# Twenty-two product units made on the spot and thirty-six from sums kept in DRAM, in place of forty-four made on the spot

## The chip, the cores and the metric

The kernel runs on one core of one Trainium2 chip. The metric is the device time of one execution in microseconds (us). Three runs of the kernel before took 2204.83, 2204.56 and 2203.43 us; the median is 2204.56 us.

A core has five engines that run their own instruction streams side by side and wait for each other through semaphores: TensorE (PE in the profile, with its weight loads as PEld), VectorE (DVE), ScalarE (ACT), GpSimd (POOL) and SyncE (SP). SP does nothing here but issue transfers (DMA) from device memory (DRAM) into the core's on-chip memory. Each engine takes its instructions strictly in the order in which they stand in its stream. Matmuls add into a second on-chip memory, PSUM.

## The reference, cut to what matters

The reference is a two-layer encoder trunk with 256 tokens and a model width of 2048, all in float32. Layer 0 mixes by neighbourhood attention, layer 1 by a gated short convolution. Each layer ends with a gated MLP of inner width 5632.

```
for i in range(2):
    a = rms_norm(h, mix_norm[i])
    if i == 0:
        q, k, v = split(a @ w_qkv, 3);  mixed = neighbourhood_softmax(q, k, v) @ w_o
    else:
        gb, gc, x = split(a @ w_in, 3); mixed = (gb * conv3(gc * x)) @ w_out
    h = h + mixed
    g, u = split(conv3(rms_norm(h, ffn_norm[i]) @ w_up) + conv_b, 2)
    h = h + (silu(g) * u) @ w_down
out = rms_norm(h, final_norm)
```

What counts for the time is nine large products with weights: `w_qkv` (q and k part `wqk`, v part `wv`), `w_o`, twice `w_up` and `w_down`, `w_in` (`wsc`) and `w_out` (`wscout`).

## The kernel before, in words

**Three matmuls for one product.** TensorE multiplies in the rounded form fp32r. To keep float32 accuracy, `parts` splits every weight chunk of 128x1024 numbers into a rounded part `hi` (ScalarE, line 139) and the rest `lo` (VectorE, line 140), and the activations are kept as such pairs too. A product is then hi·hi + hi·lo + lo·hi.

**Two kinds of stages.** In the stages `Phase` (q and k, `w_up`, `w_in`) the weights are stationary: an item is two tiles of 128 outputs, each over sixteen k tiles from two weight chunks. Line 185 does hi weights against both parts of the activation (512 wide) and line 193 lo weights against the hi part (256 wide). With `intro=3` the first three outputs are done one chunk at a time, so that the stage can start on the first eight k tiles of its input. In the stages `Tokens` (`w_o`, `w_down`, `w_out`) the activations are stationary and the weights move, 512 wide, in two groups `g` of eight output tiles. A pair of k tiles in a group is a 2x2 problem of 128 tokens by 512 outputs.

**Eight products or seven.** A plain pair does its 2x2 problem in eight products (`product`, lines 375 to 377, three matmuls each). A unit of seven does it in seven, in the manner of Strassen (`seven`): it needs sums of activations (`make_forms`, on GpSimd) and of weights (`sums`, lines 149 to 152: four VectorE additions of 128x512, then the split). Four of its products collect in four PSUM accumulators `mu`; at the end of a group `combine` (lines 409 to 417) folds those into the residual stream `h`. The plans at the top of the file say in which order the pairs of a group come and which are units of seven: 44 in all, ten in each first half of an MLP, seven in each second half, six in `w_out`, four in `w_o`.

**What sets the order.** The program text emits the work item by item. All weight chunks of the whole program stand in one list, `chunks`; `prep_to` loads them on SP through a ring of five buffers `raw` and splits them into six buffers `hi` and six `lo`, four chunks ahead of the item that TensorE works on (`AHEAD`). Per engine the instructions are then put into an order at build time, by the due times that the framework reckons, and this order is fixed when the kernel runs.

**The hand-overs.** After `w_o`, after the first layer's MLP and after `w_out` a `Tokens` stage ends and a `Phase` stage follows that needs the normalized result. `to_norm` adds the last groups into `h` (line 273), takes their squares, transposes `h` on TensorE (line 284), scales it to the new activations `a` (ScalarE line 225, VectorE line 226), works out the reciprocal root of the mean square (`token_factor`, lines 260 to 269 and 290 to 294) and spreads it over the partitions (`spread_factor`: line 300 on TensorE, line 301 copies it to `rstd`). Meanwhile TensorE does the intro items of the next stage with the eight k tiles that are ready, and it needs a8 to a15, the last eight, to go on. The last stage ends in `finale` and the final norm (`last_evac`).

Of the kernel before, what the change touches and what calls it, by code (L numbers as in the profile page):

```python
# [22 lines left out]
P = 128  # L23
# [20 lines left out]
S_FIRST = ((ORDER, (1, 3, 5, 7, 9), 3), ((0, 2, 1, 4, 3, 6, 5, 8, 7, 10, 9), (1, 3, 5, 7, 9), 6))  # L44

S_SECOND = (((0, 2, 1, 4, 3, 6, 5, 8, 7, 9, 10), (1, 3, 5, 7), 1), (ORDER, (3, 5, 7), 1))
S_OUT = (1, 3, 5)
S_ATT = (((0, 1, 2, 6, 3, 7, 4, 5), (6, 7), 1),) * 2
# [19 lines left out]
def trunk(ctx, tc, xT, par, bias, wqk, wv, wo, wsc, wscout, wup, wdown, out):  # L68
# [8 lines left out]
    ep = ctx.enter_context(tc.tile_pool(name="ends", bufs=1))  # L77

# [35 lines left out]

    def prep_to(n):
        while len(prepped) < min(n, len(chunks)):
            src, w, kind = chunks[len(prepped)]
            raw = wp.tile([P, CH * P], F32, name="raw", tag="raw", bufs=5)
            if kind == "rows":
                nc.sync.dma_start(out=raw[:, :w], in_=src)  # L120
                prepped.append(parts(raw[:, :w]) + (raw,))
                continue

            nc.sync.dma_start(out=raw.rearrange("p (f c) -> p f c", f=4), in_=src.rearrange("f p c -> p f c"))
            r = raw.rearrange("p (f k c) -> p f k c", f=4, c=P)
# [17 lines left out]
    def sums(l, r):  # L143

        t13 = wp.tile([P, CH * P], F32, name="raw", tag="raw", bufs=5)
        t24 = tp.tile([P, CH * P], F32, name="t24", tag="qk")
        v13, v24 = (x.rearrange("p (k f c) -> p f k c", f=4, c=P) for x in (t13, t24))
# [3 lines left out]
        add(out=v24[:, :, 0, :], in0=v13[:, :, 0, :], in1=r[:, :, 1, :])  # L151
        add(out=v24[:, :, 1, :], in0=v24[:, :, 0, :], in1=l[:, :, 1, :])  # L152
        return parts(r[:, :, 1:2, :]), parts(t13), parts(t24)

    class Phase:
# [3 lines left out]
        def __init__(self, w, fts, nk, src, evac, intro=0, step=CH):  # L159
# [8 lines left out]
            for two, ks in order:  # L168
# [4 lines left out]
                ends.append(len(chunks))  # L173

# [128 lines left out]
    class Tokens:  # L303
# [4 lines left out]
        def __init__(self, w, nk, src, evac, plan, forms, halves=0):  # L308
# [4 lines left out]
            for g, (order, sset, _) in enumerate(plan):  # L313
                for i in order:
# [3 lines left out]
                    if g == KT // 8 - 1 and k >= nk - halves:  # L318
# [3 lines left out]
                        chunks.extend(((left, 8 * P, "cols"), (right, 8 * P, "cols")))  # L322
                        continue
                    chunks.append((left, 8 * P, "cols"))
                    if i in sset:
                        chunks.append((right, 8 * P, "sums"))
                        items.append((self, g, c + 1, k, k, k + 2))
                        ends.append(c + 2)
                    else:
                        chunks.append((right, 8 * P, "cols"))  # L330
# [48 lines left out]
        def seven(self, g, c, k0):  # L379
# [7 lines left out]
            left, (w22, t13, t24) = prepped[c - 1], prepped[c]  # L387
# [3 lines left out]
            for ps, x, w, j in ((a, raw(0, 0), left, 0), ("11", raw(1, 0), left, 1), ("12", s4, w22, 0),  # L391
                                (e, s1, t13, 0), (f, s3, t13, 1), (b, s2, t24, 0), ("21", raw(1, 1), t24, 1)):
# [28 lines left out]
    def make_forms(xe, xo, place=None):  # L421

        if place is None:
            n = form_at[0] = (form_at[0] + 1) % 5
            y = tp.tile([P, 8 * P], F32R, name="sf", tag=("sf", "vv", "sf", "vv", "qk")[n], bufs=2)
            place = y[:, :4 * P], y[:, 4 * P:]
# [164 lines left out]
    def sc_evac(f, ps):  # L591
# [11 lines left out]
        else:  # L603
# [3 lines left out]
            if j % 2 == 0:  # L607
                sc_of["even"] = t
            elif j // 2 in S_OUT:
                yforms[j // 2] = make_forms(sc_of["even"], t)  # L610
# [113 lines left out]
    def mlp(layer, a, evac):  # L724
        for half in range(2):
            act, forms = [None] * HALF, {}
            lo = half * HALF
            Phase(wup[layer], [f for j in range(lo, lo + HALF) for f in (2 * j, 2 * j + 1)], KT, a, up_evac(layer, act, forms, (S_SECOND if half else S_FIRST)[0][1]),
                  intro=0 if half else 3)
            Tokens(wdown[layer, half], HALF, act, evac if half else residual, S_SECOND if half else S_FIRST, forms,  # L730
                   halves=4 if half and layer else 0)

    for g in range(NH // 4):
        Phase(wqk, range(8 * g, 8 * g + 8), KT, a0, qk_evac, intro=0 if g else INTRO, step=STEP)
        Values(g, a0)
    Tokens(wo, KT, oT, to_norm(1, a1), S_ATT, oforms)
    mlp(0, a1, to_norm(2, a2))
    Phase(wsc, range(3 * KT), KT, a2, sc_evac, intro=3)
# [136 lines left out]
```

## Time and profile before

| | us |
|---|---|
| median of 3 runs | 2204.56 |
| lowest and highest run | 2203.43, 2204.83 |
| profiled execution, span from first to last instruction | 2203.5 |

Stages, by the timeline of TensorE:

| stage | kind | from, to (us) | units of seven |
|---|---|---|---|
| q, k, v and attention, four groups | Phase with values and softmax between | 0 to 309 | none |
| `w_o` | Tokens | 309 to 395 | 4 |
| MLP of layer 0 | Phase, Tokens, Phase, Tokens | 395 to 1116 | 10 and 7 |
| `w_in` | Phase | 1116 to 1378 | none |
| `w_out` | Tokens | 1378 to 1470 | 6 |
| MLP of layer 1 | Phase, Tokens, Phase, Tokens | 1470 to 2190 | 10 and 7 |

The page of the profile covers one execution. Times are in microseconds unless marked ns. A row of groups names line, engine, operation and tile, then the count, the busy time, the mean time of one, and the idle time of the engine just before them with what ended it. A row of the timeline gives start, duration, engine, line, operation and operands, and in brackets the idle time before it. Matmuls overlap, so a row of eight of them takes less than eight times a single one's duration.

### The profile page before, as it was taken

To read this page: it belongs to the slowest core of one execution; us is meant where nothing else is said; L and a number is where in the kernel's file an instruction comes from. 1 tells how busy PE (TensorE), PEld (TensorE's weight loads), DVE (VectorE), ACT (ScalarE), POOL (GpSimd) and SP (SyncE) were. 2 spreads that over 40 slices of the span, in tenths; PEclk is the share of its full clock that TensorE was granted. 3 is DMA by queue.
4 is the path that set the end of the run, shared out by engine and by line. 5 is a ranking of instruction groups with operands and counts; after the bars stand their busy time and mean duration, and the time that the engine had idled before them with its cause. 6 is when DMAs were issued, how large, how long until landed. Compare 5 with 4: busy or idle time off the path is not lost.

```text
span 2203.5 us, 31950 instructions
## 1 busy us (share of the span) xinstructions
PE 2191.7 (99%) x11776; PEld 1900.1 (86%) x11776; DVE 1752.7 (80%) x2677; ACT 1274.6 (58%) x1900; POOL 71.4 (3%) x115
## 2 busy tenths in 40 slices
PE   9999999999999999999999999999999999999998
PEld 8888888888888888888888888888888888888886
DVE  8777678877788987778876666898777898777887
ACT  7555556665655565565555445566556556665554
POOL 0000000000000000000000000000000000000000
PEclk9999999999999999999999999999999999999999
DMA  7565546555556755555665555565555566555564
GB/s 259 191 198 180 172 150 211 190 191 191 191 172 196 226 200 186 191 190 185 200 196 189 187 191 183 174 224 180 190 187 184 177 212 219 191 191 192 170 203 134
DMA packets 214605, 421.00 MB, mean 191 GB/s; under 512 B 13488, under 2 KB 142640, under 8 KB 214448
## 3 DMA queue, kind: packets, MB, share of 16 engines
q1 hardware_dynamic: 213072, 418.33, 58.4%
q8 instruction: 92, 1.51, 0.3%
q10 hardware_dynamic: 1376, 0.63, 0.1%
q14 instruction: 65, 0.53, 0.1%
HBM read 416.81 MB, written 2.10 MB: 190 GB/s over the span
## 4 chain that ended last, share of the span: by engine, by line
PE 96%; DVE 1%; DMA 1%; ACT 1%; issue 0%; SPq 0%; DVEq 0%; ACTq 0%
PE mm L185 41%; PE mm L193 22%; PE mm L375 8%; PE mm L376 8%; PE mm L377 8%; PE mu L375 2%; PE mu L377 2%; PE mu L376 2%; PE mm L570 1%; PE mm L572 1%; PE mm L571 1%; DMA raw<-in_wqk 1%; PE tr L284 1%; DVE lo L140 0%; PE tr L525 0%
## 5 line engine op out<-in xcount | busy, mean ns | idle before, releaser
L140 DVE TENSOR_TENSOR lo<-raw,hi 128x1024 fp32r<-128x1024 f32 (+1 forms) x836 | 973.1, 1186 | 188.3 <-PE mm L193 123.4
L139 ACT CAST hi<-raw 128x1024 fp32r<-128x1024 f32 (+1 forms) x836 | 845.7, 1019 | 368.9 <-PE mm L377 121.8
L185 PE MATMUL mm<-a,hi 128*128 128x512 f32 x4096 | 961.7, 391 | 0.9 <-ACT hi L139 0.4
L185 PEld LDWEIGHTS mm<-a,hi 128*128 128x128 f32 x4096 | 759.2, 188 | 153.8 <-DVE a L226 2.0
L193 PEld LDWEIGHTS mm<-a,lo 128*128 128x128 f32 x4096 | 512.9, 192 | 11.9
L193 PE MATMUL mm<-a,lo 128*128 128x256 f32 x4096 | 518.0, 283 | 0.0
L375 PE MATMUL mm<-hi,act 128*128 128x512 f32 x696 | 271.4, 390 | 0.0
L376 PE MATMUL mm<-lo,act 128*128 128x512 f32 x696 | 271.1, 389 | 0.0
L377 PE MATMUL mm<-hi,act 128*128 128x512 f32 x696 | 270.8, 389 | 0.0
L238 ACT COPY corr<-mm 128x256 f32<-128x256 f32 x256 | 94.8, 372 | 240.0 <-PE mm L193 240.0
L254 DVE SCALAR_TENSOR_TENSOR conv<-pad,pt,conv 128x256 f32<-128x256 f32 x384 | 184.8, 482 | 43.8 <-ACT conv L252 28.8
L252 ACT ACTIVATE conv<-pad,pt 128x256 f32<-128x256 f32 x176 | 105.6, 601 | 145.8 <-DVE pad L244 145.8
L377 PEld LDWEIGHTS mm<-hi,act 128*128 128x128 f32 x696 | 130.6, 188 | 27.2
L375 PEld LDWEIGHTS mm<-hi,act 128*128 128x128 f32 x696 | 130.7, 188 | 26.8
L376 PEld LDWEIGHTS mm<-lo,act 128*128 128x128 f32 x696 | 130.7, 188 | 26.6
L239 DVE TENSOR_TENSOR corr<-mm,corr 128x256 f32<-128x256 f32 x256 | 106.9, 418 | 2.0 <-ACT corr L238 1.9
L218 DVE TENSOR_TENSOR act<-conv,act 128x256 fp32r<-128x256 f32 x88 | 37.4, 425 | 85.8 <-ACT act L217 85.8
L244 DVE TENSOR_TENSOR pad<-corr,rstd 128x256 f32<-128x256 f32 x176 | 74.0, 421 | 0.1
L139 ACT CAST hi<-t 128x1024 fp32r<-128x1024 f32 x44 | 46.4, 1054 | 39.6 <-DVE t L152 26.5
L140 DVE TENSOR_TENSOR lo<-t,hi 128x1024 fp32r<-128x1024 f32 x44 | 53.8, 1222 | 4.8 <-ACT hi L139 3.7
L149 DVE TENSOR_TENSOR raw<-raw 128x512 f32<-128x512 f32 x44 | 30.4, 690 | 33.2 <-DMA raw<-in_wdown 28.9
L570 PE MATMUL mm<-hi,a 128*128 128x512 f32 x128 | 50.5, 394 | 0.0
(157 smaller groups left out, 1464.0 us busy)
## 6 DMA issues: line engine op xcount, KB each, us to landing
raw<-in_wup SPq DMA_DIRECT2D x352, 512.0 KB, 4.9
raw<-in_wdown SPq DMA_DIRECT2D x176, 512.0 KB, 4.5
raw<-in_wsc SPq DMA_DIRECT2D x96, 512.0 KB, 4.9
raw<-in_wqk SPq DMA_DIRECT2D x56, 512.0 KB, 4.7
raw<-in_wv SPq DMA_DIRECT2D x32, 512.0 KB, 4.5
raw<-in_wo SPq DMA_DIRECT2D x32, 512.0 KB, 4.5
raw<-in_wscout SPq DMA_DIRECT2D x32, 512.0 KB, 4.4
raw<-in_wqk SPq DMA_DIRECT2D x16, 256.0 KB, 5.1
```

The lines of the kernel that those rows point to most:

```text
L139: nc.scalar.copy(out=hv, in_=r)
L140: nc.vector.tensor_sub(out=lv, in0=r, in1=hv.bitcast(F32))
L185: nc.tensor.matmul(self.ps[ft], lhsT=prepped[i][0][:, o:o + P], rhs=self.src[k], start=k == 0, stop=False)
L193: nc.tensor.matmul(self.ps[ft][:, S:], lhsT=prepped[i][1][:, o:o + P], rhs=self.src[k][:, :S], start=False, stop=k == self.nk - 1)
L238: nc.scalar.copy(out=corr, in_=ps[:, S:])
L239: nc.vector.tensor_add(out=corr, in0=ps[:, :S], in1=corr)
L244: nc.vector.tensor_mul(out=dst, in0=both(ps), in1=rstd)
L252: nc.scalar.activation(c, x[:, 1:S + 1], AF.Identity, scale=w[1], bias=b)
L254: nc.vector.scalar_tensor_tensor(out=c, in0=x[:, tap:tap + S], scalar=w[tap], in1=c, op0=ALU.mult, op1=ALU.add)
L375: nc.tensor.matmul(ps, lhsT=xh, rhs=wh, start=start, stop=False)
L376: nc.tensor.matmul(ps, lhsT=xh, rhs=wl, start=False, stop=False)
L377: nc.tensor.matmul(ps, lhsT=xl, rhs=wh, start=False, stop=stop)
```

## The change

There are 58 units of seven in place of 44, in two kinds. Twenty-two ("S") make their weight sums on the spot as before; their second sum tile is now written back into the right chunk's buffer in place of a tile of its own. Thirty-six ("D") take sums that were made earlier. Each half of a D unit's sums is a **job**: one load of 512 KB on SP, four additions of 128x2x128 in place on VectorE, and two stores of 256 KB on ScalarE's queue, which are issued when three more chunks have been prepared. The jobs stand in the chunk lists of the `Phase` stages: four in each group of q and k but the first, twelve in each `w_up` stage, twenty in `w_in`, 72 in all, spread evenly over the items. Their results lie in DRAM until the `Tokens` stage loads them, two chunks of 512 KB each, which are split like weights; of the pair's own right chunk it then loads half.

```
+def plan(text, due):
+    words = text.split()
+    return (tuple(int(x[1:]) for x in words), {int(x[1:]): x[0] for x in words if x[0] != "P"}, due)
-S_FIRST = ((ORDER, (1, 3, 5, 7, 9), 3), ((0, 2, 1, 4, 3, 6, 5, 8, 7, 10, 9), (1, 3, 5, 7, 9), 6))
-S_SECOND = (((0, 2, 1, 4, 3, 6, 5, 8, 7, 9, 10), (1, 3, 5, 7), 1), (ORDER, (3, 5, 7), 1))
-S_OUT = (1, 3, 5)
-S_ATT = (((0, 1, 2, 6, 3, 7, 4, 5), (6, 7), 1),) * 2
+S_FIRST = (plan("P0 D1 P2 S3 D4 P5 D6 S7 P8 D9 P10", 3), plan("P0 P2 D1 S3 D4 P5 D6 S7 P8 P10 D9", 6))
+S_SECOND = (plan("P0 P2 D1 S3 D4 P5 D6 S7 D8 P9 P10", 1), plan("P0 P1 P2 D3 S4 P5 D6 S7 D8 P9 P10", 1))
+S_OUT = (plan("P0 D1 P2 S3 D4 D5 P6 P7", 1),) * 2
+QK_JOBS, UP_JOBS, SC_JOBS = 4, 12, 20
+S_ATT = (plan("P0 P1 P2 S6 P3 S7 P4 P5", 1),) * 2
...
     def prep_to(n):
...
+            while stores and stores[0][0] <= len(prepped):
+                stores.pop(0)[1]()
             raw = wp.tile([P, CH * P], F32, name="raw", tag="raw", bufs=5)
+            if kind == "make":
+                make(raw, src, w)
+                prepped.append(())
+                continue
+            if kind in ("rows", "kept"):
+                nc.sync.dma_start(out=raw[:, :w], in_=src if kind == "rows" else src().rearrange("p m f c -> p (m f c)"))
...
     def sums(l, r):
-        add(out=v24[:, :, 0, :], in0=v13[:, :, 0, :], in1=r[:, :, 1, :])
-        add(out=v24[:, :, 1, :], in0=v24[:, :, 0, :], in1=l[:, :, 1, :])
-        return parts(r[:, :, 1:2, :]), parts(t13), parts(t24)
+        w22 = parts(r[:, :, 1:2, :])
+        add(out=r[:, :, 1, :], in0=v13[:, :, 0, :], in1=r[:, :, 1, :])
+        add(out=r[:, :, 0, :], in0=r[:, :, 1, :], in1=l[:, :, 1, :])
+        return w22, parts(t13), parts(r)
+    def make(raw, job, half):
+        w, g, i = job
+        nc.sync.dma_start(out=raw.rearrange("p (m n) -> p m n", m=4),
+                          in_=w[8 * g + half:8 * g + 8:2, :, 2 * i * P:(2 * i + 2) * P].rearrange("m p n -> p m n"))
+        l, r = (x.rearrange("p (f k c) -> p k f c", f=2, k=2) for x in (raw[:, :4 * P], raw[:, 4 * P:]))
+        add = nc.vector.tensor_add
+        add(out=l[:, 0], in0=l[:, 0], in1=r[:, 0])
+        add(out=r[:, 0], in0=r[:, 1], in1=r[:, 0])
+        add(out=r[:, 1], in0=l[:, 0], in1=r[:, 1])
+        add(out=l[:, 1], in0=r[:, 1], in1=l[:, 1])
+        if half == 0:
+            kept[id(w), g, i] = dp.tile([P, 2, 4, 2, P], F32, name=f"kept{len(kept)}")
+        dst = kept[id(w), g, i]
+        for j in range(2):
+            stores.append((len(prepped) + 3, lambda j=j: nc.scalar.dma_start(
+                out=dst[:, j, :, half, :], in_=raw.rearrange("p (m k c) -> p k m c", m=4, k=2)[:, j])))
...
     class Phase:
-            for two, ks in order:
+            made = 0
+            for n, (two, ks) in enumerate(order):
...
+                while made < len(jobs) * (n + 1) // len(order):
+                    chunks.append((*jobs[made], "make"))
+                    made += 1
...
     class Tokens:
-                    if i in sset:
-                        chunks.append((right, 8 * P, "sums"))
+                    if kinds.get(i) == "S":
+                        chunks.append((right, 2 * P, "sums"))
...
+                    elif i in kinds:
+                        chunks.append((right[:, :, P:], P, "cols"))
+                        chunks.extend((lambda j=j, key=(id(w), g, i): kept[key][:, j], 8 * P, "kept") for j in range(2))
```

How this moves instructions is seen best at three places. The first is VectorE at the hand-over from `w_o` to the first `w_up` stage. Before, its rows from the last two residual additions to the copy of `rstd` stand like this (lo<-raw,hi splits a weight chunk, a<-tr,pt,a makes one of the tiles a8 to a15):

```order
L273 TENSOR_TENSOR h<-mm,h 128x512 x2
L140 TENSOR_TENSOR lo<-raw,hi 128x1024 x3
L226 SCALAR_TENSOR_TENSOR a<-tr,pt,a 128x256
L290 TENSOR_REDUCE z<-ssq_106 128x2
L140 TENSOR_TENSOR lo<-raw,hi 128x1024
L226 SCALAR_TENSOR_TENSOR a<-tr,pt,a 128x256 x2
L260 TENSOR_SCALAR z<-z 128x2
L140 TENSOR_TENSOR lo<-raw,hi 128x1024
L226 SCALAR_TENSOR_TENSOR a<-tr,pt,a 128x256 x2
L266 RECIPROCAL m<-m 128x2
```

Of the changed kernel, the rows behind those in which a9 to a12 are made, on the same engine at the same place (raw<-raw, lines 182 to 185, are the additions of a job, here the third):

```order
L278 SCALAR_TENSOR_TENSOR a<-tr,pt,a 128x256 x2
L185 TENSOR_TENSOR raw<-raw 128x2x128
L158 TENSOR_TENSOR lo<-raw,hi 128x1024
L278 SCALAR_TENSOR_TENSOR a<-tr,pt,a 128x256 x2
L318 RECIPROCAL m<-m 128x2
L182 TENSOR_TENSOR raw<-raw 128x2x128
L319 TENSOR_TENSOR m<-m 128x2
L183 TENSOR_TENSOR raw<-raw 128x2x128
L278 SCALAR_TENSOR_TENSOR a<-tr,pt,a 128x256 x2
L320 SCALAR_TENSOR_TENSOR m<-m,z 128x2
L184 TENSOR_TENSOR raw<-raw 128x2x128
L321 SCALAR_TENSOR_TENSOR rcol<-m 128x2
```

Eleven additions of three jobs now stand between the last residual addition and the factor's last step; the third job's first two stand ahead of a13 and a14, its fourth ahead of a15. Nothing of the kind stood there before.

The second place is TensorE at the same hand-over, from the first matmul that needs a8 (a_4076 before, a_4177 in the changed kernel) on; mm_4048 and mm_4149 are the first output tile of the stage, mm_4115 and mm_4216 the second, and a13 is a_4101 before and a_4202 now. Before:

```order
L185 MATMUL mm_4048<-a_4098,hi_4044 128x512
L185 MATMUL mm_4115<-a_4076,hi_4067 128x512
L185 MATMUL mm_4115<-a_4079,hi_4067 128x512
L185 MATMUL mm_4115<-a_4087,hi_4067 128x512
L185 MATMUL mm_4115<-a_4090,hi_4067 128x512
L185 MATMUL mm_4115<-a_4098,hi_4067 128x512
L185 MATMUL mm_4154<-a_4076,hi_4134 128x512
L185 MATMUL mm_4048<-a_4101,hi_4044 128x512
```

In the changed kernel:

```order
L237 MATMUL mm_4149<-a_4199,hi_4168 128x512
L237 MATMUL mm_4149<-a_4202,hi_4168 128x512
L237 MATMUL mm_4216<-a_4177,hi_4235 128x512
L237 MATMUL mm_4149<-a_4210,hi_4168 128x512
L237 MATMUL mm_4216<-a_4180,hi_4235 128x512
L237 MATMUL mm_4216<-a_4188,hi_4235 128x512
L237 MATMUL mm_4216<-a_4191,hi_4235 128x512
```

Ahead of both pieces stand the four matmuls of the first tile with a8 to a11. The matmul with a13 was the twelfth from a8 and is now the sixth.

The third place is SP in the first `w_down` stage, where before 44 loads in_wdown of 128x4x256 followed one another. Now the loads of the kept sums and of the half right chunks (128x4x128) stand between them:

```order
L142 DMA raw<-in_wdown 128x4x256 x3
L142 DMA raw<-in_wdown 128x4x128
L138 DMA raw<-kept_1178 128x1024 x2
L142 DMA raw<-in_wdown 128x4x256 x5
L142 DMA raw<-in_wdown 128x4x128
L138 DMA raw<-kept_1458 128x1024 x2
```

For a D unit four loads are issued in place of two, and SP's queue has them in the order in which VectorE and ScalarE split them.

60 lines of the change are left out of this document (39 added, 21 removed).

## The prediction

> **What bounds the kernel now.** The page's busy times come first, then what TensorE waits for, then the stages.
>
> ```profile
> PE 2191.7 (99%) x11776; PEld 1900.1 (86%) x11776; DVE 1752.7 (80%) x2677; ACT 1274.6 (58%) x1900; POOL 71.4 (3%) x115
> PE bc L686 <- DVE conv L684: 1.6, 1, 1.6
> PE tr L669 <- DVE h L273: 0.8, 1, 0.8
> PE mm L185 <- DVE a L226: 0.4, 1, 0.4
> 497.51 7.28 PE mm L185 x32
> ```
>
> TensorE is busy 99% of the span, and its longest wait is 1.6 us, in the tail. So the time is TensorE's list of matmuls, and a matmul less is time less, as long as no new wait appears. The last row, from the chain of waits, prices one of 512 columns: 7.28 / 32 = 0.2275 us (the 0.39 us of a single matmul overlaps its neighbours). A product of three takes 0.6825 us, a plain pair of eight 5.46 us, a unit of seven 4.78 us.
>
> The windows show how much room the others have, in the order: stretch, length, PE, PEld, DVE, ACT, POOL, clock, DMA share, GB/s. They are most of the first `w_up` stage (425), a first and a second `w_down` stage (642, 1000), `w_in` (1140), and one group of q and k (83).
>
> ```profile
> 425.00:640.00 215.00, 215.00 (x1242) 190.54 (x1241) 170.43 (x280) 128.87 (x199) 10.60 (x20) 1.00 0.56 184
> 642.00:752.00 110.00, 110.00 (x486) 91.04 (x486) 98.59 (x120) 61.42 (x68) 0.00 (x0) 1.00 0.67 205
> 1000.00:1122.00 122.00, 122.00 (x560) 101.70 (x559) 103.43 (x129) 71.09 (x92) 0.00 (x0) 1.00 0.66 205
> 1140.00:1378.00 238.00, 238.00 (x1370) 210.62 (x1369) 160.43 (x247) 118.41 (x161) 7.59 (x12) 1.00 0.56 187
> 83.00:158.00 75.00, 75.00 (x425) 65.82 (x424) 53.58 (x89) 41.33 (x73) 4.07 (x4) 1.00 0.58 184
> ```
>
> VectorE is the next bound: 90% in `w_down`, 67 to 79% in the Phase stages.
>
> **What goes.** Fourteen more units of seven are 14 products, 42 matmuls fewer in TensorE's order. 42 x 0.2275 = **-9.55 us**, all on the path, since PE is busy through every stage's window.
>
> **What the jobs cost inside the Phase stages.** Groups of VectorE, and what it waits for:
>
> ```profile
> L140 DVE TENSOR_TENSOR lo<-raw,hi 128x1024 fp32r<-128x1024 f32 x776 | 935.5, 1224 | 184.4 <-PE mm L193 123.4 <-ACT hi L139 52.2 <-issue 5.8
> L629 DVE TENSOR_TENSOR conv<-conv,g 128x256 f32<-128x256 f32 x88 | 37.4, 425 | 8.1
> 2190.39 2.07 DVE L692 TENSOR_TENSOR a<-a,bc 128x256 f32<-128x256 f32 x6
> L150 DVE TENSOR_TENSOR raw<-raw 128x512 f32<-128x512 f32 x44 | 30.1, 685 | 0.0
> DVE raw L149 <- DMA raw<-in_wdown: 28.9, 21, 3.2
> ```
>
> A job's addition has 256 numbers a partition, like L629: at most 0.425 us, or 2.07 / 6 = 0.345 where six follow one another (L692), so 1.4 to 1.7 us a job. By 1.7, twelve jobs lift `w_up` from 170 to 191 of 215 us, twenty lift `w_in` from 160 to 194 of 238, four lift a group of q and k from 54 to 60 of 75. All stay under TensorE. Each addition can also wait for its load, as L149 does (28.9 us in 21 times, 1.4 each), and then what is queued behind it on VectorE waits: splits, conv, sums. What hides that: the splits wait 123.4 us for TensorE to free a `lo` buffer, so they run ahead of need, and `w_up` has 24 us of VectorE idle left against 12 x 1.4 = 17. I take **0**. If the cover were gone, each job could cost 1.4 us, 17 us a `w_up` stage; of that I keep 0 to 3 us for the range, since 7 us of idle stay over in the tightest stage. Seven more sets of activation sums add a split of 0.69 us each (VectorE) and work for GpSimd, which is 3% busy: 0.
>
> The stores and loads:
>
> ```profile
> L693 ACTq DMA_DIRECT2D out<-a x4: 378/387/409, 2197.9 to 2199.9; - x4
> raw<-in_wup SPq DMA_DIRECT2D x352, 512.0 KB, 4.9
> raw<-in_wdown SPq DMA_DIRECT2D x176, 512.0 KB, 4.5
> raw<-in_wqk SPq DMA_DIRECT2D x16, 256.0 KB, 5.1
> out<-a ACTq DMA_DIRECT2D x4, 128.0 KB, 2.3
> ```
>
> 144 store issues at 0.39 us are 56 us on ScalarE, which is busy 58%: 0. A store of 256 KB is not in the trace; it lies between 2.3 us (128 KB written) and 4.9 us (512 KB read). I take 3: the job's buffer is held that long, of five. SP issues 144 loads more (72 jobs, and 4 in place of 2 for each of 36 D units); it does nothing else, and a late one is counted below.
>
> **What the kept loads cost in the Tokens stages.** VectorE is relieved where D takes the place of S: four additions of 0.685, 2.74 us. In the first `w_down` stage 98.6 falls to about 86 us; in the second it stays at 103. The load moves to the transfers: a D unit brings 1.835 MB in 4.78 us, a plain pair 1.049 MB in 5.46. A first stage comes to 14 x 1.049 + 8 x 1.835 = 29.4 MB in 112 us, 262 GB/s, against 205 seen; D S D in a row needs 4.72 MB in 14.3 us, 329. The start of the kernel is the fastest that the trace shows:
>
> ```profile
> 0.00:20.00 20.00, 18.03 (x100) 15.74 (x101) 13.44 (x28) 15.25 (x37) 0.37 (x7) 1.00 0.83 277
> ```
>
> So 262 has been reached, 329 hasn't. With five buffers and loads that land in 5.0 us the tightest place, S7 followed by D8 (four times, all in second stages), has 0.7 to 0.9 us left; at 5.5 us it stalls 0.3 each time, and each further us costs about 1.2 there, and at other D units from 6 us on. I take **+0.5** (0 to 6). The Trainium skill, "DMA: Bandwidth & Descriptors", Specifications, puts a core's limit at about 358 GB/s; by it 329 would pass and this term be 0 to 1; no run here shows such a rate.
>
> **The hand-overs.** Here VectorE is the path. The first one before, VectorE's rows, then ScalarE's and TensorE's:
>
> ```profile
> 393.96 0.69 DVE L273 TENSOR_TENSOR h<-mm,h 128x512 f32<-128x512 f32 x1
> 394.94 0.69 DVE L273 TENSOR_TENSOR h<-mm,h 128x512 f32<-128x512 f32 x1 [0.29 <-PE mm L377]
> 395.55 3.49 DVE L140 TENSOR_TENSOR lo<-raw,hi 128x1024 fp32r<-128x1024 f32 x3
> 402.38 1.22 DVE L140 TENSOR_TENSOR lo<-raw,hi 128x1024 fp32r<-128x1024 f32 x1 [0.88 <-ACT hi L139]
> 403.52 0.87 DVE L226 SCALAR_TENSOR_TENSOR a<-tr,pt,a 128x256 fp32r<-128x256 f32 x2
> 406.94 0.87 DVE L226 SCALAR_TENSOR_TENSOR a<-tr,pt,a 128x256 fp32r<-128x256 f32 x2
> 408.36 0.48 DVE L226 SCALAR_TENSOR_TENSOR a<-tr,pt,a 128x256 fp32r<-128x256 f32 x1 [0.54 <-ACT a L225]
> ...
> 403.10 1.28 ACT L261 ACT_TABLE_LOAD   x1
> ...
> 404.84 4.29 PE L185 MATMUL mm<-a,hi 128*128 128x512 f32 x17
> 408.99 0.67 PE L300 MATMUL st<-conv,ones 128*128 128x256 f32 x2
> ```
>
> TensorE starts on a8 at 404.84 and takes one matmul per 0.2275 us. Before, a13 was the twelfth, at 407.3, and was made at 407.3. In the new order it is the sixth, wanted at 404.84 + 5 x 0.2275 = 405.98. VectorE's new order, with 0.35 us per job addition, 1.14 per split (3.49 for three) and 0.40 per `a`: the fourth residual ends at 396.4, since a split now stands ahead of it. A split, the rest of jobs 1 and 2 and a8 (ScalarE's part is ready at 400.4) bring it to the sixth chunk's split at 402.6. That chunk is late itself: its load waited for the third chunk's split (394.0) and 4.9 us. Its split frees the buffer for job 3's load, 4.5 us: 407.1. VectorE comes to job 3's first addition at 405.9 and waits. Two additions and two small steps later a13 is made at 408.3: TensorE stalls **2.3**. The factor then comes at 410.75, 0.3 after TensorE wants it: 2.7 with rounding. Lower end: if job 3's load lands before VectorE gets there, 1.3; upper end, landing 6.4 us: 4.6.
>
> The second and third hand-over have the same rows 721.16 and 1075.44 us later:
>
> ```profile
> 1116.10 0.69 DVE L273 TENSOR_TENSOR h<-mm,h 128x512 f32<-128x512 f32 x1 [0.29 <-PE mm L377]
> 1126.00 4.29 PE L185 MATMUL mm<-a,hi 128*128 128x512 f32 x17
> 1480.28 4.19 PE L185 MATMUL mm<-a,hi 128*128 128x512 f32 x17
> ```
>
> In the second four jobs stand in the intro, but job 3's additions come early, and only the fourth is among a13 to a15: a13 at 1127.3 against 1126.00 + 1.14, 0.2; a15 0.7 late; factor 0.5: **1.4** (1 to 5, the upper end if job 4's load, which waits for job 1's stores, is 3 us later). In the third, two jobs stand ahead of the factor: a13 at 1482.65 against 1481.42, 1.25, and 0.5 for the factor, **1.7** (1 to 3). Together **+5.8** (3.5 to 12).
>
> **The tail.** Row of the last residual, and the window around it:
>
> ```profile
> 2193.46 0.69 DVE L273 TENSOR_TENSOR h<-mm,h 128x512 f32<-128x512 f32 x1 [0.75 <-PE mm L377]
> 2160.00:2203.00 43.00, 34.66 (x159) 27.48 (x157) 31.04 (x63) 19.69 (x36) 0.00 (x0) 0.93 0.41 123
> ```
>
> The last unit is now D8, right ahead of the finale, and no plain pair covers combine's eight additions (8 x 0.685 = 5.5 us); they fall among the finale's residuals: **+0.8** (0 to 1.5).
>
> **Sum.** -9.55 + 0 + 0.5 + 5.8 + 0.8 = **-2.45 us**: from the profiled span of 2203.5 to about 2201.0. The median of the runs is 1.06 us above that span, which is what lies around it; 2204.56 - 2.45 = **2202.1 us**. A measurement tells about 0.2%, 4.4 us, from no change: faster is below 2200.15, slower above 2208.97.
>
> **The rivals.**
> - *All hidden* (2195.8): VectorE's order is the same, but loads land before they are wanted and job 3 doesn't stop it, so only -9.55 and the tail's 0.8 count. For: the windows' room, and before, the same hand-over cost 0.4 us. Against: eleven additions ahead of the factor, and a13 wanted 1.4 us earlier. 0.30.
> - *Slower, by late loads* (2212): stores and loads together stretch a load from 4.9 to 6.5 us. Then Tokens stages lose 5.8 and hand-overs 5 more: -9.55 + 5.8 + 5.8 + 5 + 0.8 = +7.9. It decides from about 6 us. For: 329 GB/s is beyond any window. Against: at 277 GB/s, in the start, the loads of `wqk` of 256 KB landed in 5.1 us. 0.16.
> - *TensorE's clock* (2210): with 8.3 us idle in the tail's 43 us the clock is 0.93 there, 3 us lost, 0.36 per us idle; elsewhere it is 1.00. If each of the three hand-overs stalls 3.4 us or more, that is 10.2 + 3.7 - 9.55 + 1.3 = +5.7. Against: my stalls come in pieces of 2.3 us at most. The Trainium skill, "TensorE: Matmul & The Clock Gate", Part 1, has the clock halve after an idle window of some 3.4 us; the 0.93 row agrees in direction. 0.04.
> - That the change removes fewer matmuls than it says is excluded by TensorE's order.
>
> **How the numbers follow.** My forecast, hand-overs that eat much of the gain, has 0.50 and covers 2199 to 2208. A fifth of it lies below 2200.15: faster is 0.30 + 0.10 = 0.40. The last two rivals make slower 0.20, the rest, 0.40, is the same. The range reaches to 2195.5, under the all-hidden case, and to 2212.5, over the late loads; about 0.15 is left out.
>
> **What would show it.** PE's busy sum falls by 9.55 us. PE's waits name the first product's `mm` behind VectorE's `a`, 4 to 6 us at three places, and VectorE's first job addition waits for in_wdown. Kept loads land in 4.5 to 5 us; over 6 would be the late-load case, with PE waits in the Tokens windows. No waits of PE at the hand-overs would make me wrong towards 2196; PE waits inside the Phase stages would make the 0 there wrong.

## The result, and the profile after

| | before | changed |
|---|---|---|
| median of the runs, us | 2204.64 | 2295.25 |
| lowest and highest, us | 2203.43, 2204.83 | 2284.41, 2301.93 |
| profiled execution, span, us | 2203.5 | 2282.6 |

The ratio is 1.0406 (95% interval 1.0376 to 1.0436): **4% slower**, 91 us, where 2.45 us less was forecast. The profiled execution is the fastest of the four runs (2284.41), 79.1 us over before. The page of the changed kernel, its busy times and its chain:

```profile
PE 2213.9 (97%) x11734; PEld 1903.5 (83%) x11734; DVE 1828.5 (80%) x2912; ACT 1277.0 (56%) x1935; POOL 89.5 (4%) x143
PE 50%; DMA 22%; DVE 17%; ACT 5%; issue 4%; POOL 1%; SPq 0%; ACTq 0%; DVEq 0%
```

The 42 matmuls are gone (11776 to 11734), yet TensorE's busy time rose by 22.2 us. The chain, 96% TensorE before, now runs half of the span through transfers, VectorE and ScalarE. What TensorE waits for (engine, line, releaser: us in total, times, longest), and what VectorE and SP wait for:

```profile
PE mm L432 <- DVE corr L291: 21.9, 4, 6.9
PE o L595 <- DVE act L270: 8.8, 3, 5.1
PE mm L237 <- DVE a L278: 8.1, 5, 3.7
PE mu L433 <- DVE lo L158: 7.2, 10, 0.8
PE mm L245 <- DVE lo L158: 4.0, 4, 1.9
...
DVE raw L182 <- DMA raw<-in_wdown: 41.7, 44, 3.2
DVE lo L158 <- PE mm L245: 25.6, 18, 3.8
...
SPq L138 <- DMA kept<-raw: 144.8, 52, 6.7
```

All of TensorE's rows together are 61.6 us, against 5.3 before. The row to look at is the lo split that waits for TensorE: this is time in which VectorE has split further ahead than the six `lo` buffers hold. It was 123.4 us before and is 25.6 now; the lead is used up. The last row is SP: 52 times a load stood behind a job's store that had not landed, and every later load stood behind that one. ScalarE now waits for the weights of `w_up`, where before it hardly did (before first, then changed):

```profile
ACT hi L139 <- DMA raw<-in_wup: 12.6, 17, 2.3
ACT hi L157 <- DMA raw<-in_wup: 101.4, 97, 4.1
```

The transfers themselves (KB each, median us to landing) are little slower than before, where w_up took 4.9:

```profile
raw<-in_wup SPq DMA_DIRECT2D x352, 512.0 KB, 5.1
...
kept<-raw ACTq DMA_DIRECT2D x144, 256.0 KB, 3.0
raw<-kept SPq DMA_DIRECT2D x72, 512.0 KB, 5.1
```

TensorE's clock is the second part. The granted clock and a window at the largest kind of wait:

```profile
core 0: 2282.6 us, clock 0.989
664.30:671.00 6.70, 4.33 (x10) 3.46 (x11) 6.70 (x12) 3.11 (x6) 0.00 (x0) 0.50 0.62 200
671.00:680.00 9.00, 9.00 (x41) 7.38 (x41) 8.54 (x13) 4.62 (x7) 0.00 (x0) 1.00 0.38 116
```

Along the span the clock is at 0.50 in nine spells of 3.4 or 6.8 us among the matmuls, 44.2 us in all, which is 22.1 us of clock. Some 4 of these fall into the waits themselves (the first window above begins 2.4 us before its wait ends), so about 18 us are lost to matmuls. Before, the only spell begins with TensorE's last matmul, at 2196.7 us, and costs next to nothing. So the 79.1 us are -9.55 (matmuls) + 56.3 (waits) + about 18 (clock), and some 14 in longer steps from one matmul to the next, which I have not assigned. That is not idle time: all but 1 us of TensorE's idle time is in the list.

Where it goes shows by stage. The table gives us from the last weight matmul of the stage ahead to the last one of the stage, worked out from the starts of TensorE's matmuls, for the kernels that matter below. The first row is counted from 23.3 us on, and `w_o`, 89.1 us in each, is left out. The 72 jobs run out early: the last `w_up` stage has four of them, one every 55 to 67 us, and not twelve as the text on the change says.

| stage | before | changed | jobs only | units only | no load | no stores | seven raw |
|---|---|---|---|---|---|---|---|
| q, k, v | 282.1 | 294.4 | 293.4 | 281.5 | 285.6 | 292.5 | 285.9 |
| w_up 1 | 247.2 | 252.2 | 251.5 | 247.2 | 246.8 | 252.3 | 246.8 |
| w_down 1 | 112.8 | 122.2 | 116.8 | 114.3 | 115.1 | 112.8 | 113.8 |
| w_up 2 | 244.6 | 253.8 | 253.6 | 244.6 | 245.2 | 244.6 | 244.6 |
| w_down 2 | 116.6 | 128.5 | 126.5 | 118.7 | 116.6 | 122.0 | 115.6 |
| w_in | 269.4 | 275.4 | 273.9 | 270.9 | 269.1 | 270.3 | 273.8 |
| w_out | 84.9 | 95.5 | 89.2 | 85.6 | 84.9 | 84.9 | 83.4 |
| w_up 3 | 247.0 | 248.0 | 248.4 | 247.9 | 247.0 | 249.0 | 247.9 |
| w_down 3 | 112.8 | 122.2 | 121.3 | 114.0 | 112.8 | 112.8 | 112.5 |
| w_up 4 | 244.6 | 244.6 | 244.6 | 244.6 | 244.6 | 244.6 | 244.6 |
| w_down 4 | 118.7 | 122.0 | 118.7 | 122.2 | 118.7 | 118.7 | 116.0 |

The largest waits, 4 to 7 us, stand at the starts of four Tokens stages. The first of them, TensorE's row, then ScalarE's and VectorE's in the time ahead of it:

```profile
666.67 0.80 PE L432 MATMUL mm<-hi,act 128*128 128x512 f32 x1 [4.60 <-DVE corr L291]
...
662.74 1.04 ACT L157 CAST hi<-raw 128x1024 fp32r<-128x1024 f32 x1 [1.49 <-DMA raw<-kept]
664.00 1.04 ACT L157 CAST hi<-raw 128x1024 fp32r<-128x1024 f32 x1
664.95 0.64 ACT L290 COPY corr<-mm 128x256 f32<-128x256 f32 x2
...
664.47 1.82 DVE L158 TENSOR_TENSOR lo<-raw,hi 128x1024 fp32r<-128x1024 f32 x2
666.21 0.41 DVE L291 TENSOR_TENSOR corr<-mm,corr 128x256 f32<-128x256 f32 x1
```

TensorE needs the PSUM buffer that the last outputs of the Phase stage still occupy. What empties it (`corr`, ScalarE, then VectorE) stands in the fixed order behind splits of later chunks: before as now it stands behind 237 lo splits, but it came 1.0 us into the stage and comes 8.8 us into it now. That order was laid out for splits that are long done by then; now they wait for their loads, and the emptying waits with them.

### The profile page after: what moved, and what is told of

It is laid out like the page before. It is cut to its first block, busy times and chain, and to the rows that moved or that the text cites. A ratio compares the mean times of both kernels' runs of the same rounds, so it can differ in the third digit from the quotient of the medians.

```text
span 2282.6 us, 32819 instructions
## 1 busy us (share of the span) xinstructions
PE 2213.9 (97%) x11734; PEld 1903.5 (83%) x11734; DVE 1828.5 (80%) x2912; ACT 1277.0 (56%) x1935; POOL 89.5 (4%) x143
## 2 busy tenths in 40 slices
DMA packets 339027, 524.88 MB, mean 230 GB/s; under 512 B 18096, under 2 KB 257840, under 8 KB 338864
## 4 chain that ended last, share of the span: by engine, by line
PE 50%; DMA 22%; DVE 17%; ACT 5%; issue 4%; POOL 1%; SPq 0%; ACTq 0%; DVEq 0%
PE mm L237 24%; PE mm L245 12%; DMA raw<-in_wdown 9%; DVE lo L158 9%; DMA raw<-in_wsc 4%; ACT hi L157 4%; PE mm L432 3%; PE mm L433 3%; PE mm L434 3%; DMA raw<-in_wup 3%; DMA raw<-in_wscout 2%; DMA raw<-kept 1%; DMA kept<-raw 1%; DVE conv L306 1%; DMA raw<-in_wqk 1%
## 5 line engine op out<-in xcount | busy, mean ns | idle before, releaser
L157 ACT CAST hi<-raw 128x1024 fp32r<-128x1024 f32 (+1 forms) x908 | 911.2, 1013 | 533.4 <-DMA raw<-in_wup 101.4
L158 DVE TENSOR_TENSOR lo<-raw,hi 128x1024 fp32r<-128x1024 f32 (+1 forms) x908 | 1050.9, 1178 | 137.1 <-ACT hi L157 107.6
L432 PE MATMUL mm<-hi,act 128*128 128x512 f32 x612 | 243.3, 397 | 22.3 <-DVE corr L291 21.9
L433 PE MATMUL mm<-lo,act 128*128 128x512 f32 x612 | 242.3, 396 | 1.7 <-DVE lo L158 1.5
L434 PE MATMUL mm<-hi,act 128*128 128x512 f32 x612 | 241.3, 394 | 0.0
L432 PEld LDWEIGHTS mm<-hi,act 128*128 128x128 f32 x612 | 116.8, 191 | 50.0 <-DVE corr L291 24.0
L433 PEld LDWEIGHTS mm<-lo,act 128*128 128x128 f32 x612 | 117.0, 191 | 28.1 <-DVE lo L158 4.3
L434 PEld LDWEIGHTS mm<-hi,act 128*128 128x128 f32 x612 | 116.7, 191 | 24.4
L290 ACT COPY corr<-mm 128x256 f32<-128x256 f32 x256 | 87.0, 368 | 56.1 <-PE mm L245 55.6
L182 DVE TENSOR_TENSOR raw<-raw 128x256 f32<-128x256 f32 x72 | 30.5, 423 | 55.3 <-DMA raw<-in_wdown 41.7
L433 PE MATMUL mu<-lo,sf 128*128 128x512 f32 x162 | 65.0, 401 | 7.6 <-DVE lo L158 7.2
L432 PE MATMUL mu<-hi,sf 128*128 128x512 f32 x162 | 63.8, 394 | 3.9 <-DVE a L278 2.6
L434 PE MATMUL mu<-hi,sf 128*128 128x512 f32 x162 | 63.2, 390 | 0.0
```

The lines of the kernel that those rows point to most:

```text
L157: nc.scalar.copy(out=hv, in_=r)
L158: nc.vector.tensor_sub(out=lv, in0=r, in1=hv.bitcast(F32))
L290: nc.scalar.copy(out=corr, in_=ps[:, S:])
L432: nc.tensor.matmul(ps, lhsT=xh, rhs=wh, start=start, stop=False)
L433: nc.tensor.matmul(ps, lhsT=xh, rhs=wl, start=False, stop=False)
L434: nc.tensor.matmul(ps, lhsT=xl, rhs=wh, start=False, stop=stop)
```

## The experiments

Each number is one execution with its profile, but for `e12`, `e17` and `e18`. The changed kernel's own runs spread over 17.5 us, so single runs that differ by less are told apart by their stages, not by their total. Before, beside them, took 2204.4 to 2205.7 us.

**Jobs only** (`e1_jobs_only`), **units only** (`e2_units_only`), **stores on GpSimd** (`e3_stores_gpsimd`), **jobs in the middle of the stages** (`e4_jobs_mid`):

```
# jobs only: the plans of before for the Tokens stages, the jobs of the changed kernel for the Phase stages
+J_FIRST, J_SECOND, J_OUT, J_ATT = S_FIRST, S_SECOND, S_OUT, S_ATT     # for plan_jobs
+S_FIRST = (plan("P0 S1 P2 S3 P4 S5 P6 S7 P8 S9 P10", 3), ...
# units only
-chunks.extend((lambda j=j, key=(id(w), g, i): kept[key][:, j], 8 * P, "kept") for j in range(2))
+chunks.extend((wup[0][8 * i + 4 * g + j, :, :8 * P], 8 * P, "rows") for j in range(2))
# stores on GpSimd
-stores.append((len(prepped) + 3, lambda j=j: nc.scalar.dma_start(
+stores.append((len(prepped) + 3, lambda j=j: nc.gpsimd.dma_start(
# jobs in the middle: n0 = 2 * intro + 1 (0 without intro), n1 = len(order) - 2
-while made < len(jobs) * (n + 1) // len(order):
+while made < len(jobs) * max(0, min(n, n1) + 1 - n0) // (n1 + 1 - n0):
```

> All 72 jobs of the changed kernel in its Phase stages, but the Tokens stages as before: 44 units of seven, all summed on the spot, so no kept sums are loaded. Theory 1 (the jobs block the queues: VectorE's first addition waits for its load, ScalarE's store waits for the additions, and in-order work behind both is late): the losses seen in the changed kernel's Phase stages and at the starts of the Tokens stages stay, some 33 + 22 us, so 2245 to 2265. Theory 2 (the loads of kept sums in the Tokens stages are what is late): only the hand-overs cost, 8 us, so 2210 to 2217, and no wait of TensorE over 2 us at the start of a Tokens stage.

Measured: 2262.65 us, 57 over before. Theory 1 it is, by number: the jobs alone bring most of the loss, and the waits at the starts of the Tokens stages come although no kept sum is loaded there.

> The 58 units of the changed kernel, but no jobs; the two kept chunks of each D unit are replaced by two chunks of w_up of the same size, so the loads, splits and matmuls of the Tokens stages are all there and only the values are others. Theory 1: the waits inside the Tokens stages (some 15 us) are all that is left beside the gain of 9.55, so 2200 to 2212, and none at the starts of the stages. Theory 2: Tokens stages 45 us longer in all than before, so about 2250.

Measured: 2216.81 us, 11 over before, so with the 9.55 that its 42 matmuls save, the change of units costs about 20 us by itself (it loads other weights in place of the kept sums, so its values are others). That lies between the two theories, nearer to the first. No wait at the start of any Tokens stage; the rows of TensorE that are left stand inside:

```profile
PE mu L433 <- DVE lo L158: 5.9, 9, 0.8
PE mu L432 <- DVE a L278: 1.8, 2, 0.9
```

> The changed kernel with the jobs' stores issued on GpSimd's queue in place of ScalarE's. If ScalarE, held behind a store that waits for the additions, is what makes casts and evacuations late (theory 1a), the waits of 4 to 7 us at the starts of the Tokens stages and the 5.3 us in the first group with jobs go: 2235 to 2260. If VectorE, held behind the additions that wait for their load, is enough (theory 1b), less than 10 us goes: 2275 to 2300.

Measured: 2289.23 us. ScalarE's queue is not the cause; theory 1a falls.

> The changed kernel with the jobs kept out of the intro items of each Phase stage and off its last item (none behind the last two items). If the job right ahead of the Tokens stage makes its start late, the four waits of 4 to 7 us go with their half-clock spells, and the hand-overs' 8 us too: 2284 - 22 - 10 - 8 - 3 = about 2240. If the D unit that stands second or third in the stage does it, with its four loads, the starts keep their waits: 2270 to 2290.

Measured: 2295.18 us, a little over the second number. The starts keep their waits (5.0, 6.0, 3.5 and 5.0 us), so it is not the last job that makes them. What is won there is lost elsewhere: the second w_up, where the jobs stand almost as before, takes 261.4 us against 253.8, and why is open. But the waits of the hand-overs go, 8.1 us to 2.0, as the rows for the same pair show:

```profile
PE mm L239 <- DVE a L280: 2.0, 5, 1.0
```

**A job without its load, without its additions, on GpSimd, and with late additions** (`e5` to `e8`; the first two are edits of jobs only):

```
# no load: the dma_start of make is left out, the additions read h
-add(out=l[:, 0], in0=l[:, 0], in1=r[:, 0])
+add(out=l[:, 0], in0=x[0], in1=x[1])          # x: four slices of h; so for all four
# no additions: the four calls of add are left out
# on GpSimd: add = nc.gpsimd.tensor_add, and stores by nc.gpsimd.dma_start
# late additions: the four calls stand in a function sum_up, called two chunks later
+stores.append((len(prepped) + 2, sum_up))
```

> The run with jobs only, without the jobs' loads: the four additions read the residual stream, which stands ready, write the job's buffer, and the stores stay; the kept values are not used there. Theory 1b (what hurts is that VectorE's first addition waits for its load): the 57 us over before shrink to under 10, so 2205 to 2215, and no wait of TensorE over 2 us at the starts of the Tokens stages. Rival (VectorE's time alone, 72 x 1.7 = 122 us, uses up the lead of its splits): 2240 to 2260.

Measured: 2210.96 us, 6 over before. VectorE still does all 288 additions, so its time is not the cost. Nor do SP's waits behind the stores measure the loss: they are more than twice those of the changed kernel here.

```profile
SPq L142 <- DMA kept<-raw: 338.7, 64, 9.2
```

> The run with jobs only, without the jobs' additions: load and two stores of the loaded data are left, VectorE has no part in a job. Theory 1b: under 10 us over before, 2205 to 2215. Rival (the buffer of five that a job holds through load and store, 8 us or more, makes the next weight loads late): 2225 to 2260.

Measured: 2278.85 us, 74 over before, with no job instruction on VectorE at all. Theory 1b, which the run before seemed to show, falls here: VectorE's wait for the job's load isn't needed for the loss. The row of the lead does not tell the two runs apart either: VectorE's wait for TensorE ahead of the lo split is 36.2 us without the load, where 6 are lost, and 36.6 here. What differs is how long a job holds its buffer; the table under `e9` has the times.

> The changed kernel with the jobs' additions and stores on GpSimd, so that nothing of a job stands in VectorE's or ScalarE's order. Theory 1b: the Phase stages and the starts of the Tokens stages lose nearly nothing, and what is left is the waits inside the Tokens stages: 2284 - 33 - 22 - 15 of clock = 2210 to 2225. Rival (buffers): an addition on GpSimd takes about 1 us, a job's buffer is held some 12 us, and it is 2260 or slower.

Measured: 2408.16 us. The buffer is held longest here (a median of 12.9 us from the job's load to the landing of its second store, against 11.2 in the changed kernel), and SP's wait for the stores is four times that of the changed kernel:

```profile
SPq L138 <- DMA kept<-raw: 565.4, 64, 12.5
```

> The changed kernel with the additions of a job written two chunks later than its load, so that the load has landed when VectorE comes to them; the buffer is held longer. Theory 1b: 2235 to 2260, since the waits for in_wdown and in_wscout go and the starts are on time. Rival (buffers): no better than 2284, or slower.

Measured: 2288.35 us: no better, the rival's number. But the run does not decide between the two. The additions hardly moved in the order that was built: VectorE waits 43.1 us in 42 times for loads of in_wdown, against 41.7 in 44.

**Theory 3: the ring.** A job takes one of five `raw` buffers. By the order of issues, the median from a job's load to the issue of its second store is 8.6 us, and to that store's landing 11.2 us. While it lasts four buffers serve the weights, and SP, in order, cannot pass the load that is to reuse the job's buffer. Runs `e9` to `e12`:

```
# no stores: the two stores.append of make are left out
# own buffers: only in w_in, where 6 of 22 activation tiles are free; two loads, four stores
+two = [act_tile().bitcast(F32) for _ in range(2)] if raw is None else (raw[:, :4 * P], raw[:, 4 * P:])
# half the jobs
+if made % 2 == 0:
     chunks.append((*jobs[made], "make"))
# few: 49 units, 26 jobs at chosen items
+S_FIRST = (plan("P0 D1 P2 S3 D4 P5 D6 S7 P8 D9 P10", 3), plan("P0 P2 S1 P5 S4 P8 S6 P7 S3 P10 S9", 6))
+S_SECOND = (plan("P0 P2 S1 P4 S3 P6 S5 P8 S7 P9 P10", 1), plan("P0 D1 P2 S3 P4 S5 P6 S7 P8 P9 P10", 1))
+S_OUT = (plan("P0 D1 P2 S3 D4 D5 P6 P7", 1), plan("P0 S1 P2 S3 P4 S5 P6 P7", 1))
```

> The run with jobs only, without the jobs' stores: load and additions stay, and the buffer is free as soon as the additions are done. Theory 3a (a job's buffer is held too long, above all by the stores, which are issued three chunks later and land 3 us after that): most of the 57 us go, 2205 to 2220. Theory 3b (the job's load itself, one more load of 5 us through the same ring, and VectorE's wait for it): 2235 to 2260.

Measured: 2229.46 us, 25 over before: between the two numbers. Three of the four starts are clean; q and k and the hand-overs are not, where VectorE comes to a job's addition ahead of its load.

Side by side, with the median time for which a job holds its buffer (from the issue of its load, or from its first addition where there is no load, to the landing of its second store, or to the end of its last addition where there are no stores):

| run | buffer held, us | over before, us |
|---|---|---|
| no load | 5.7 | 6 |
| no stores | 7.6 | 25 |
| jobs only | 11.2 | 57 |
| no additions | 11.1 | 74 |

The loss grows with the time that the buffer is held. The last two differ by about as much as the changed kernel's own runs do.

> The run with jobs only, but the twenty jobs of the w_in stage use two free activation tiles each in place of a buffer of the ring, with two loads of 256 KB and four stores of 128 KB; all other stages are as they were. If the ring of five is the cause, the w_in stage falls from 273.9 us to 270 or less and the w_out stage behind it from 89.2 to 85, TensorE's waits at its start gone. If it is VectorE's in-order wait for the loads, both stay within 1.5 us.

Measured: 2262.03 us; w_in 273.0, w_out 90.7. The ring's number is missed, and that of VectorE's wait for the loads is met. But the edit made this wait longer, so it doesn't count fully against the ring either: VectorE waited 37.8 us in 12 times for the loads into these tiles, up to 5.0 each. From 1190 to 1420 us that is 34.9, against 12.4 for the jobs' loads with jobs only, while ScalarE's wait for weights of `w_in` fell from 91.8 to 35.5:

```profile
DVE act L194 <- DMA act<-in_wdown: 29.9, 10, 4.4
DVE act L194 <- DMA act<-in_wscout: 7.9, 2, 5.0
```

> The run with jobs only, with every second job left out (36 of 72). If each job costs a fixed piece, half of the 57 us stays: about 2233. If jobs cost because the lead of the loads isn't won back before the next one (theory 3), it is well under half, 2205 to 2222, with the w_up stages without intro at 245 us.

Measured: 2211.11 us, 6.7 over before, and the second w_up at 244.6. Half of the jobs cost about an eighth of what all cost, which no fixed price per job gives. VectorE's lead is back, in the row of the lo split:

```profile
DVE lo L162 <- PE mm L250: 80.7, 47, 4.4
```

> A version meant to beat both: 49 units, of which 13 take kept sums, only where the run with units alone showed no wait; 26 jobs, none in the q and k groups, none in an intro, none behind the last four items of a stage. Five units more than before are worth 5 x 0.6825 = 3.4 us. Theory 3 with lead won back: 2201 to 2203. If any job costs: 2208 or more.

Measured: 2207.93 us (2205.41 to 2209.41, 10 runs), ratio 1.0016 (1.0006 to 1.0025). That is 3.5 over before and the number of the other case, in which a job costs. Five more units gain nothing; the hoped-for number is missed by some 5 us.

**More buffers.** Only the numbers of buffers are changed in the program; 6 + 5 takes the memory of 5 + 6. The build lays out the engines' order anew, and it differs in places. `e13` and `e14` have six raw and five lo, `e15` the same on the kernel before, `e16` seven raw, five hi and five lo on the changed kernel:

```
-raw = wp.tile([P, CH * P], F32, name="raw", tag="raw", bufs=5)
+raw = wp.tile([P, CH * P], F32, name="raw", tag="raw", bufs=6)
-lo = wp.tile([P, CH * P], F32R, name="lo", tag="lo", bufs=6)
+lo = wp.tile([P, CH * P], F32R, name="lo", tag="lo", bufs=5)
```

> The run with jobs only, with six buffers for raw weights and five for the lo parts, in place of five and six (the same memory). Theory 4 (a job's buffer, held through load, additions and stores, leaves the weight loads too few of the five, and the lead of the splits wears off): 57 us over before fall to under 20, 2207 to 2225, and TensorE's waits at the starts of the Tokens stages go. Theory 5 (the fixed order with VectorE's waits for the job loads is what costs, the ring is not): 2245 to 2265.

Measured: 2244.78 us, 39 over before in place of 57: a third of the loss goes, and the number is that of theory 5. By stages it is mixed: q, k, v (280.7), the first w_up (247.6) and w_out (85.1) are back, the second w_up is not (256.3), and the starts of the first three w_down stages wait 2.1, 8.0 and 5.7 us.

> The changed kernel with six raw and five lo buffers. Theory 4: the stages with jobs recover as in the run before, and the Tokens stages with D units too, since their waits came from the same ring: 2284 falls to 2200 to 2225. Theory 5: 2270 or more.

Measured: 2257.30 us. Better than every run of the changed kernel, but not the number of either theory. q, k, v fall to 281.5 and the first w_up to 247.6; the starts of the first three w_down stages still wait 5.4 to 6.9 us.

> Control: the kernel before with six raw and five lo buffers. Both theories: TensorE waited for nothing there, so it stays within 3 us of 2204.6; if it gets slower by more, one lo buffer less costs by itself and the two runs beside it are to be read against this one.

Measured: 2204.88 us. The exchange of buffers alone does nothing.

> The changed kernel with seven raw buffers and five each of hi and lo. Theory 4: no slower than with six raw buffers, 2195 to 2220, as long as five hi buffers are enough. Theory 5: 2270 or more.

Measured: 2211.42 us. With two buffers more, 84 of the 91 us are gone (73 against the fastest run of the changed kernel), although the weight loads land later than with five (5.8 us for w_up, 4.0 for the stores). The same bytes (524.88 MB) move in less time, so it was not the rate of transfers. The starts are clean, and the lead is back. The order at the starts is no rival: VectorE empties the last outputs of these four Phase stages behind 236, 392, 554 and 690 lo splits, one fewer each than in the changed kernel, but 0.9 to 1.4 us into the Tokens stage, where it was 8.3 to 11.4. SP still waits 154.6 us behind stores.

```profile
core 0: 2209.6 us, clock 0.997
DVE lo L158 <- PE mm L245: 87.4, 67, 4.5
```

**Versions meant to beat both:** seven raw buffers, no jobs in q and k or in an intro; `e18` also drops the D units of the second group of each first w_down stage.

```
-QK_JOBS, UP_JOBS, SC_JOBS = 4, 12, 20
+QK_JOBS, UP_JOBS, SC_JOBS = 0, {(0, 0): 16, (0, 1): 14, (1, 0): 12, (1, 1): 14}, 16     # 58 units
+QK_JOBS, UP_JOBS, SC_JOBS = 0, {(0, 0): 8, (0, 1): 14, (1, 0): 8, (1, 1): 10}, 16       # 56 units
+at_ = [n0 + j * (n1 - n0) // len(jobs) for j in range(len(jobs))]                       # item behind which job j stands
```

> Meant to beat both: the changed kernel with seven raw, five hi and five lo buffers, and the jobs put where the run with seven buffers showed no loss: none in the q and k groups, none in an intro, sixteen, fourteen, sixteen, twelve and fourteen in the five other Phase stages. Theory 4: the 2211 of the run with seven buffers less the 3.8 us of q and k, the 4.4 of the hand-over to w_in and 0.9 of that to the second w_up: 2202. If sixteen jobs in the first w_up stage wear its lead off even with seven buffers: 2206 to 2215.

Measured: 2211.14 us (2207.06 to 2217.17, 5 runs), ratio 1.0036 (1.0023 to 1.0050): the number of the second case. The first w_up, which that case blames, is at 247.5 us against 246.8 with seven raw buffers; the second, with fourteen jobs in place of twelve, stays at 244.6.

> The same with 56 units, 28 of them D: the second group of each first w_down stage, which kept waits of 1.5 us with D units, takes five on-the-spot units, so the first w_up stage has eight jobs. Theory 4: Phase stages as before the change, Tokens stages 6.6 us shorter in all, 2198 to 2201.

Measured: 2203.91 us (2203.00 to 2206.55, 11 runs), ratio 0.9998 (0.9989 to 1.0007): the same as before, and short of the expectation by some 3 us. Twelve products fewer are worth 8.2 us, and nothing of that shows in the median. By the stages as in the table, the Tokens stages are 5.0 us shorter in all, the three stages that begin with a hand-over together 2.6 longer. No version here beats the kernel before by what can be measured.

## Why the prediction was wrong, point by point

- *What goes, -9.55.* Right as a count. It is seen as time only where nothing waits: with seven raw buffers w_out is 1.5 us shorter for two units more.
- *Jobs inside the Phase stages, 0.* **This is the step that failed**, with the one under it: "I take 3: the job's buffer is held that long, of five". VectorE's time was counted against its idle time, and that was right: without the load the same additions cost 6 us in all. What was not counted is the buffer. The store alone took the 3 us, but a job holds its buffer 11.2 us, from its load on, while the next loads stand behind it on SP in order. In place of 0 the jobs alone cost 57 us, hand-overs included. The lead of the splits, the 123.4 us that I named as the cover, wears off faster than it is won back at one job per 22 us, as in the w_up stages; at half as many it holds. So the cover was not a stock to set 1.4 us a job against, but what the ring of five could still give. That more buffers bring the time back (2284, 2257, 2211 with five, six and seven, and nothing from the sixth on the kernel before) is shown; that the time a buffer is held sets the loss rests on four single runs, each of which also changes other things; that VectorE's wait for a job's load has a part in it is likely from the runs without load and without stores, but how the loss divides between the two stays open, since the run with buffers of its own changed both.
- *Kept loads in the Tokens stages, +0.5 (0 to 6).* Wrong in size: the run with units only lost about 20 us against their gain. Kept loads landed in 5.1 us, as assumed, and S7 followed by D8 did stall, but so did D6 followed by S7, which I had not counted: with the buffer for the sums, these two units take seven buffers of a ring of five. It is the ring again and not the rate of transfers: with seven raw buffers the waits of this kind (`mu` for a lo split) fall from 7.2 us in ten times to 2.1 in three.
- *Hand-overs, +5.8 (3.5 to 12).* Right in the sum, 7.6 us, but in part by luck: TensorE waited 3.09, 3.66 and 0.86 us for `a`, where 2.7, 1.4 and 1.7 were worked out. In the second, job 4's first addition waited 2.61 us for its load, which was my upper end there. The first one, VectorE's row and TensorE's:

```profile
420.77 0.42 DVE L182 TENSOR_TENSOR raw<-raw 128x256 f32<-128x256 f32 x1 [2.24 <-DMA raw<-in_wdown]
...
422.11 1.22 PE L237 MATMUL mm<-a,hi 128*128 128x512 f32 x2 [3.09 <-DVE a L278]
```

  Job 3's first addition waits for its load, 2.24 us, with a13 behind it, and TensorE stalls 3.09. All five waits of this kind, two of them in the start of the kernel, are 8.1 us, and without jobs in the intro they shrink to 2.0.
- *Tail, +0.8.* TensorE's wait for the residual in the tail went from 0.8 to 1.7 us; right.
- *The starts of the Tokens stages* were not looked at: 21.9 us in four waits. I took the covered splits as slack and did not ask which work stands behind them in ScalarE's and VectorE's order when they are late.
- *TensorE's clock* had 0.04. My price of 0.36 us per us idle was read from the tail's window, where the half clock begins with the last matmul and costs next to nothing. Here it cost about 18 us, and it came with shorter waits than the 3.4 us that I had set as its condition. The second wait in the q and k groups is an example, 2.19 us, and the clock in the window behind it:

```profile
178.46 0.38 PE L595 MATMUL o<-act,vv 128*128 128x256 f32 x1 [2.19 <-DVE act L270]
178.00:184.00 6.00, 5.54 (x28) 5.24 (x29) 5.20 (x10) 1.32 (x4) 0.00 (x0) 0.72 0.79 259
```

- *Slower, by late loads* (0.16) had the right sign and the wrong cause: it waited for loads to land in 6.5 us. They landed in 5.1. They were issued late, as ScalarE's waits for them show.

## What to carry to other kernels

Before work is put into the gaps of a stage, count what it holds, not only what it does: buffers of a shared ring from load to the landing of the last store, and what an in-order queue cannot pass meanwhile. A large wait of a producer for the bound engine is lead, and what wears it off does not add up job by job: test the same insertion at half the density, and watch that row. It warns, but it does not size the loss. Where the order of the engines is fixed when the kernel is built, ask of every split or cast that may come late what stands behind it.

## What the runs showed of the hardware

- Beside waits of TensorE of some 2 us and more, its granted clock was 0.50 for 3.4 or 6.8 us (nine times in the changed kernel, by the granted clock along its span). Five of these spells began while the wait still ran; of the 22.1 us of clock about 18 fell on matmuls. One spell followed a wait of 1.77 us (jobs only, clock 0.72 from 253 to 259 us), while a wait of 2.44 us in the run with jobs in the middle left the clock alone (1.00 from 179.5 to 186 us). The page of the Trainium skill, "TensorE: Matmul & The Clock Gate", Part 1, has the clock fall to half after an idle window of some 3.4 us; the length and the half agree with these runs, but spells followed waits of 1.77 and 2.19 us here.
- The loss is not proportional to the work inserted: 36 jobs cost 6.7 us, 72 cost 57.
- A store of 256 KB landed in 3.0 us (median of 144; 4.0 with seven raw buffers), between the two ends that the prediction set.
